# Taking turns between two output tiles in the matmuls of two ConvFFNs (one Trainium2 core, float32 trunk)

## The chip, the core and the metric

The kernel runs on one core of one Trainium2 chip. The metric is device time in microseconds (us), the median of several executions; lower is better. TensorE (PE) multiplies, VectorE (DVE) and ScalarE (ACT) do the elementwise work, GpSimd (POOL) a little of it, and SyncE (SP) issues the weight transfers. TensorE adds into PSUM, a memory of eight banks; one bank holds 512 float32 columns for each of the 128 partitions.

## The reference, cut to what matters

The program is a two-layer decoder trunk on 256 tokens with 2048 features. Each layer has a token mixer (an RG-LRU and RWKV-7 layer first, then an mLSTM layer) and after it a gated ConvFFN; a final RMSNorm closes it. The change is in the ConvFFN, which runs twice:

```python
def conv_ffn(x, norm, w_gate, w_up, conv_w, conv_b, w_down):
    h = rms_norm(x, norm)                                # 2048 features
    u = silu(causal_dwconv(h @ w_gate, conv_w, conv_b)) * (h @ w_up)   # 5632 features, 3 taps
    return x + u @ w_down
```

All of it is float32. The mixers and norms around it are unchanged.

## The kernel before

Activations lie feature-major: 128 features on the partitions, the 256 tokens along the free axis. So a product is a sum over k-tiles of 128 input features, and an output tile is 128 features by 256 tokens. A ConvFFN has 44 gate tiles and 44 up tiles over 16 k-tiles each (2048 = 16 x 128), and then 16 down tiles over 44 k-tiles each (5632 = 44 x 128): 88 x 16 + 16 x 44 = 2112 pairs of an output tile and a k-tile, 4224 in the two ConvFFNs.

Weights come in chunks of 1 MB, sixteen 128 x 128 weight tiles each. `chunk` (L192) has one transfer on the SP queue into a `raw` buffer, and splits it in four pieces of 512 columns into an exact high part `wh` (ACT, L201) and a low part `wl` (DVE, L202). There are two buffers of each, so a chunk is converted while the one before it is multiplied. The moving operand of a k-tile is stored in the same way, as [low | high], 2 x 256 columns. `mm3` (L205) makes the product of three float32r passes with two matmuls:

- a wide one (L214, for the first k-tile L211): `wh` against both halves, 512 columns into the whole bank of the output tile;
- a narrow one (L212): `wl` against the high half, 256 columns, into the second half of that bank.

For the first k-tile of an output tile the wide one comes first, since it opens the sum; for all others the narrow one comes first. Both add into the same bank, the tile `mm` of a pool of three banks (`psum_mm`, L220). So an output tile is one bank, filled by 32 matmuls (gate and up) or 88 (down) without another bank between, apart from a few side matmuls. In the even layer the products are made with `EWIDE` false: three narrow matmuls of 256 columns for a k-tile (L216 to L218).

`project` (L223) does one gate or up tile, one chunk each, and `projections` (L234) yields gate and up tiles in turn, the first two made ahead because the norm's factor `rstd` comes late. `ffn` (L363) takes them: `scaled` (L339) copies one half from PSUM by ACT (L350), adds the other by DVE (L351) and multiplies by `rstd` (L353); `conv` is one ACT and two DVE instructions (L332, L335); then come Silu (L375), the product (L377) and the split of the result into `ux` (L174, L175). `flat` (L241) does the down tiles; `add_residual` (L356) adds both halves of a finished tile onto the residual (L358, two DVE instructions) and, by `norm_tile`, prepares the next layer's operand (L269, L270) and sum of squares (L283, L285). `tick` lets side work emit a step; in a ConvFFN that is the norm's end (`np` tiles, L296 and L323) and, in the first, the folding of small weights on DVE.

A scheduler of the language sets the order on each engine when the program is built, and each engine runs its own list in that order, waiting on semaphores where a buffer or an operand is not there yet.

Of the kernel before, what the change touches and what calls it, by code (L numbers as in the profile page):

```python
"""Hybrid trunk: (RG-LRU | RWKV-7) layer, mLSTM layer, a gated ConvFFN after each, final RMSNorm.

Activations lie feature-major on the chip (128 features on the partitions, the 256 tokens along the
free axis), weights stream through in 1 MB chunks of sixteen 128x128 tiles.  The large products run
as three float32r passes over exact high/low parts of both operands; the small ones as plain float32.
"""
# [11 lines left out]
F32 = mybir.dt.float32  # L18
# [4 lines left out]
PSUM = bass.MemoryType.PSUM  # L23

P = 128
T = 256
D = 2048
# [35 lines left out]
NV = 0  # L63
# [43 lines left out]
class Builder:  # L107
# [20 lines left out]
    def load_x(self, gain, low, outs):  # L128
        """x, and the products with the low-rank inputs' weights as both come in; the first gain leads the queues"""
# [19 lines left out]
    def load_vec(self, gain):  # L149
        """the other vectors"""  # L150
        g = VOFF[gain]
        for lo, hi in ((0, g), (g + KD, NV)):
            if hi > lo:
                self.nc.sync.dma_start(out=self.vec_sb[:, lo:hi], in_=self.io["vec"][:, lo:hi])

# [16 lines left out]
    def split(self, src, x):  # L172
        """exact float32r parts of a float32 tile: x[:, 0] the low one, x[:, 1] the high one"""
# [31 lines left out]
    def mm3(self, ps, w, c, x, start, stop):  # L205
        """w x but for the product of the low parts; two halves [w_hi x_lo, w_hi x_hi + w_lo x_hi] where ps has them"""
# [16 lines left out]
    def project(self, src, wide=True):  # L223
        """one output tile of a product with the normalised residual, before the factor rstd"""
# [9 lines left out]
    def projections(self, src, n, wide=True):  # L234
        """the first two at once: the factor rstd comes late"""
# [5 lines left out]
    def flat(self, src, nk, nm, x, done):  # L241
        """products whose (m, k) tiles lie in one flat stream; done(m, psum) takes each result"""
# [30 lines left out]
    def square(self, k, engine=None):  # L273
        """onto the sum of squares: by the engine given, or by ScalarE and VectorE"""
# [41 lines left out]
    def row_bcast(self, psum, pool, cols, tag):  # L316
        """[128 tokens, 2] -> [128, 256]: the token's value on every partition"""
# [21 lines left out]
    def scaled(self, pool, ps, pad, tag, bufs=None):  # L339
        """psum * rstd behind pad zero columns"""  # L340
# [22 lines left out]
    def ffn(self, l, gain):  # L363
        nc, tc = self.nc, self.tc
        with ExitStack() as es:
            big = es.enter_context(self.tile_pool(name=f"ffn{l}", bufs=1))
            tmp = es.enter_context(self.tile_pool(name=f"ffnt{l}", bufs=2))
            nps = es.enter_context(self.tile_pool(name=f"ffn_ps{l}", bufs=2, space=PSUM))
            self.norm_psum = lambda: nps.tile([P, T], F32, name=self.name("np"), tag="np")
            ux = []  # L370
            ps = self.projections(self.io[f"fgu{l}"], 2 * NF)
            for f in range(NF):
                g = self.scaled(tmp, next(ps), 2, "g")
                c = self.conv(tmp, g, 3, f"f_conv_w{l}", NF, f"f_conv_b{l}", f, "cv")
                nc.scalar.activation(c, c, AF.Silu)  # L375
                u = self.scaled(tmp, next(ps), 0, "u")
# [3 lines left out]
            self.flat(self.io[f"fd{l}"], NF, KD, ux, lambda m, ps: self.add_residual(m, ps, gain))  # L380

# [1 line left out]
    def even(self, gain):  # L383
        nc, tc = self.nc, self.tc
        with ExitStack() as es:
# [8 lines left out]
            # low-rank inputs: [decay | a] and the gate  # L394
# [12 lines left out]
            # their parts [hi; lo] for decay and a; hi, lo and [hi; lo; hi] for the gate  # L407
# [9 lines left out]
            # the biases of halved arguments  # L417
# [24 lines left out]
            def parts(i):  # L442
                # the second half goes where spent tiles of y lie, to leave the next layer its operands' places
# [31 lines left out]
    def sigmoid(self, out, x, bias=0.0):  # L475
        """0.5 + 0.5 tanh(x / 2); the bias comes halved"""
# [663 lines left out]
```

## Time and profile before

| | |
|---|---|
| time, median of 3 runs | 2657.59 us (2653.79 to 2658.26) |
| span of the profiled execution | 2653.5 us, 4.1 us under the median |
| TensorE busy | 2612.7 us, 98% of the span, 16200 matmuls |
| TensorE weight loads | 2282.9 us, 86% |
| VectorE / ScalarE / GpSimd busy | 71% / 55% / 6% |
| DMA | 454.40 MB, 171 GB/s |
| mean granted TensorE clock | 0.997 of full speed |

Of the profiled execution the span is all that is shown. The page's busy time of TensorE counts from a matmul's start to its modelled end, and matmuls overlap; what a stream of matmuls really costs is read from the distance between starts, which the timeline gives to 0.01 us. PEld is the loading of the stationary operand, which overlaps the matmul before it. A wide matmul moves 512 columns and a narrow one 256.

### The profile page before, as it was taken

What the parts mean: (1) busy time and instruction counts of PE and PEld (TensorE: products, weight loads), DVE (VectorE), ACT (ScalarE), POOL (GpSimd) and SP (SyncE); (2) the same over time, 40 slices, a digit from 0 to 9 for tenths busy, and PEclk for the clock granted to TensorE, in tenths of its full rate; (3) what the DMA queues carried; (4) which work ended last, traced back from release to release, by engine and by line L of the source; (5) the groups of instructions that cost most, each with busy time, mean ns of one, the idle gap of its engine ahead of it and who ended that gap; (6) DMA issues with size and microseconds to landing.
All of it is one profiled execution on the core that took longest, in us unless ns stands there. A gap on an engine that the chain in (4) does not pass through costs nothing.

```text
span 2653.5 us, 42929 instructions
## 1 busy us (share of the span) xinstructions
PE 2612.7 (98%) x16200; PEld 2282.9 (86%) x16200; DVE 1890.9 (71%) x4251; ACT 1456.0 (55%) x3078; POOL 163.3 (6%) x442
## 2 busy tenths in 40 slices
PE   7999999999999999999999999999999999999997
PEld 7988887888888888888888888888888888888886
DVE  7988888897777776555777688865677777775554
ACT  5766674555555554444666667644455555554443
POOL 4122121000000000000000000000000000000000
PEclk9999999999999999999999999999999999999999
DMA  5433334565555555555444344455555555555553
GB/s 188 154 122 122 122 105 139 176 220 194 186 191 189 182 186 190 191 190 192 149 151 149 133 154 159 143 192 189 184 184 188 191 183 184 189 191 190 183 188 138
DMA packets 67120, 454.40 MB, mean 171 GB/s; under 512 B 9264, under 2 KB 9776, under 8 KB 13664
## 3 DMA queue, kind: packets, MB, share of 16 engines
q1 hardware_dynamic: 62352, 443.78, 47.9%
q0 software_dynamic: 4416, 7.85, 1.2%
q8 instruction: 128, 2.10, 0.3%
q14 instruction: 80, 0.66, 0.1%
q10 hardware_dynamic: 144, 0.01, 0.0%
HBM read 448.70 MB, written 2.10 MB: 170 GB/s over the span
## 4 chain that ended last, share of the span: by engine, by line
PE 81%; DVE 0%; ACT 0%; POOL 0%; issue 0%; DVEq 0%; POOLq 0%
PE mm L214 49%; PE mm L212 26%; PE mm L211 3%; PE sc L856 1%; PE pv L841 1%; PE pz L996 1%; PE pr L850 1%; PE pz L997 0%; DVE res L1041 0%; PE pz L974 0%; PE pt L323 0%; PE pt L1010 0%; PE pt L987 0%; DVE res L358 0%; PE pt L989 0%; POOL rsq L307 0%
## 5 line engine op out<-in xcount | busy, mean ns | idle before, releaser
L214 PE MATMUL mm<-x,wh 128*128 128x512 f32 x3600 | 1282.8, 397 | 0.0
L202 DVE TENSOR_TENSOR wl<-raw,wh 128x512 fp32r<-128x512 f32 (+1 forms) x1680 | 1100.6, 686 | 230.5 <-ACT wh L201 229.5
L201 ACT CAST wh<-raw 128x512 fp32r<-128x512 f32 (+1 forms) x1680 | 936.0, 616 | 406.9 <-PE mm L214 307.7
L212 PE MATMUL mm<-x,wl 128*128 128x256 f32 x3840 | 1045.8, 283 | 0.0
L214 PEld LDWEIGHTS mm<-x,wh 128*128 128x128 f32 x3600 | 676.3, 188 | 150.9
L212 PEld LDWEIGHTS mm<-x,wl 128*128 128x128 f32 x3840 | 725.2, 189 | 22.7 <-DVE yx L175 2.3
L214 PE MATMUL mm<-ux,wh 128*128 128x512 f32 x1376 | 484.4, 394 | 0.0
L212 PE MATMUL mm<-ux,wl 128*128 128x256 f32 x1408 | 390.4, 281 | 0.0
L214 PEld LDWEIGHTS mm<-ux,wh 128*128 128x128 f32 x1376 | 258.7, 188 | 59.6
L212 PEld LDWEIGHTS mm<-ux,wl 128*128 128x128 f32 x1408 | 264.0, 188 | 2.8
L214 PE MATMUL mm<-yx,wh 128*128 128x512 f32 x720 | 256.2, 395 | 0.0
L212 PE MATMUL mm<-yx,wl 128*128 128x256 f32 x768 | 210.3, 285 | 1.9 <-DVE wl L202 1.0
L216 PE MATMUL mm<-x,wh 128*128 128x256 f32 x640 | 194.5, 304 | 0.0
L218 PE MATMUL mm<-x,wl 128*128 128x256 f32 x640 | 182.9, 286 | 2.5 <-DVE wl L202 2.5
L217 PE MATMUL mm<-x,wh 128*128 128x256 f32 x640 | 181.5, 284 | 0.0
L350 ACT COPY g<-mm 128x256 f32<-128x256 f32 x88 | 32.9, 374 | 241.7 <-PE mm L214 241.7
L214 PEld LDWEIGHTS mm<-yx,wh 128*128 128x128 f32 x720 | 135.2, 188 | 28.8
L212 PEld LDWEIGHTS mm<-yx,wl 128*128 128x128 f32 x768 | 143.7, 188 | 7.8 <-DVE wl L202 1.4
L351 DVE TENSOR_TENSOR g<-mm,g 128x256 f32<-128x256 f32 x88 | 37.4, 425 | 138.5 <-ACT g L350 138.4
L216 PEld LDWEIGHTS mm<-x,wh 128*128 128x128 f32 x640 | 122.3, 191 | 6.9
L218 PEld LDWEIGHTS mm<-x,wl 128*128 128x128 f32 x640 | 122.5, 191 | 3.5 <-DVE wl L202 2.8
L217 PEld LDWEIGHTS mm<-x,wh 128*128 128x128 f32 x640 | 123.0, 192 | 0.4
(349 smaller groups left out, 2461.4 us busy)
## 6 DMA issues: line engine op xcount, KB each, us to landing
raw<-fgu SPq DMA_DIRECT2D x176, 1024.0 KB, 4.8
raw<-fd SPq DMA_DIRECT2D x88, 1024.0 KB, 4.8
raw<-oin SPq DMA_DIRECT2D x64, 1024.0 KB, 4.8
raw<-ein SPq DMA_DIRECT2D x40, 1024.0 KB, 4.9
raw<-oout SPq DMA_DIRECT2D x32, 1024.0 KB, 4.8
raw<-eoa SPq DMA_DIRECT2D x8, 1024.0 KB, 5.0
raw<-eob SPq DMA_DIRECT2D x8, 1024.0 KB, 4.9
wif<-wif POOLq DMA_DIRECT2D x12, 256.0 KB, 3.3
```

What stands on the lines that cost most here:

```text
L201: nc.scalar.copy(hi[:, s], raw[:, s])
L202: nc.vector.tensor_tensor(out=lo[:, s], in0=raw[:, s], in1=hi[:, s].bitcast(F32), op=ALU.subtract)
L211: TE.matmul(ps, hi, x, start=True, stop=False)
L212: TE.matmul(ps[:, 1], lo, x[:, 1], start=False, stop=False)
L214: TE.matmul(ps, hi, x, start=False, stop=stop)
L216: TE.matmul(ps, hi, x[:, 0], start=start, stop=False)
L217: TE.matmul(ps, hi, x[:, 1], start=False, stop=False)
L218: TE.matmul(ps, lo, x[:, 1], start=False, stop=stop)
L350: nc.scalar.copy(r, ps[:, 0])
L351: nc.vector.tensor_tensor(out=r, in0=ps[:, 1], in1=r, op=ALU.add)
L841: TE.matmul(ps[:, s], xm[:, 3 + s * P:3 + s * P + P], bv, start=True, stop=True)
L850: TE.matmul(ps, bl, xc, start=True, stop=True)
```

## The change

The two ConvFFNs no longer use `projections` and `flat`. A new `flat_pairs` makes two output tiles at a time: the gate and the up tile of the same 128 features, or two neighbouring down tiles. Their PSUM tile is two banks (`[P, 2, 2, T]`, 512 float32 columns for each output tile), from a pool of two such tiles, four banks; the pool of the norm's `np` tiles shrinks from two banks to one. A chunk now holds 8 k-tiles of both output tiles, so the layout of the weights in memory is changed to match on the host; its size and its number are the same. For a k-tile `mm3_pair` issues the two wide matmuls, one into each bank, and then the two narrow ones, one into each bank. The results of a pair are taken out together when the pair is done.

```diff
+    def mm3_pair(self, ps, w, c, x, start, stop):
+        TE = self.nc.tensor
+        hi = [w[0][:, i:i + P] for i in c]
+        lo = [w[1][:, i:i + P] for i in c]
+        for i in range(2):
+            TE.matmul(ps[:, i], hi[i], x, start=start, stop=False)
+        for i in range(2):
+            TE.matmul(ps[:, i, 1], lo[i], x[:, 1], start=False, stop=stop)
+
+    def flat_pairs(self, src, nk, npair, x, pool):
+        w, ps = None, None
+        for i in range(npair * nk):
+            k = i % nk
+            if i % 8 == 0:
+                w = self.chunk(src[i // 8])
+            if k == 0:
+                ps = pool.tile([P, 2, 2, T], F32, name=self.name("mp"), tag="mp")
+            c = i % 8 * 2 * P
+            self.mm3_pair(ps, w, (c, c + P), x[k], k == 0, k == nk - 1)
+            if i % 2 == 1:
+                self.tick()
+            if k == nk - 1:
+                yield ps
...
     def ffn(self, l, gain):
...
-            nps = es.enter_context(self.tile_pool(name=f"ffn_ps{l}", bufs=2, space=PSUM))
+            nps = es.enter_context(self.tile_pool(name=f"ffn_ps{l}", bufs=1, space=PSUM))
+            pps = es.enter_context(self.tile_pool(name=f"ffn_pp{l}", bufs=2, space=PSUM))
...
-            ps = self.projections(self.io[f"fgu{l}"], 2 * NF)
-            for f in range(NF):
-                g = self.scaled(tmp, next(ps), 2, "g")
+            pairs = self.flat_pairs(self.io[f"fgu{l}"], KD, NF, self.x, pps)
+
+            ahead = [next(pairs) for _ in range(2)]
+            for f, ps in enumerate(chain(ahead, pairs)):
+                g = self.scaled(tmp, ps[:, 0], 2, "g")
                 c = self.conv(tmp, g, 3, f"f_conv_w{l}", NF, f"f_conv_b{l}", f, "cv")
                 nc.scalar.activation(c, c, AF.Silu)
-                u = self.scaled(tmp, next(ps), 0, "u")
+                u = self.scaled(tmp, ps[:, 1], 0, "u")
...
-            self.flat(self.io[f"fd{l}"], NF, KD, ux, lambda m, ps: self.add_residual(m, ps, gain))
+            for m, ps in enumerate(self.flat_pairs(self.io[f"fd{l}"], NF, KD // 2, ux, pps)):
+                for i in range(2):
+                    self.add_residual(2 * m + i, ps[:, i], gain)
```

What the built programs have in a row shows the change at three places. First TensorE in the gate-and-up part of the first ConvFFN, where one output tile ends and the next begins, as it was (`mm` is an output tile's bank, `x` the operand of a k-tile, `wh` and `wl` the parts of the weights):

```order
L214 MATMUL mm_1505_9998<-x_1136_6750,wh_1503_9988 128x512
L212 MATMUL mm_1505_9998<-x_1139_6775,wl_1504_9989 128x256
L214 MATMUL mm_1505_9998<-x_1139_6775,wh_1503_9988 128x512
L211 MATMUL mm_1511_10051<-x_1073_6317,wh_1509_10041 128x512
L212 MATMUL mm_1511_10051<-x_1073_6317,wl_1510_10042 128x256
L212 MATMUL mm_1511_10051<-x_1076_6341,wl_1510_10042 128x256
L214 MATMUL mm_1511_10051<-x_1076_6341,wh_1509_10041 128x512
L212 MATMUL mm_1511_10051<-x_1082_6378,wl_1510_10042 128x256
```

and as it is now (`mp` is the tile of two banks; x2 is one matmul into each of them):

```order
L263 MATMUL mp_1493_10132<-x_1139_6775,wh_1495_10167 128x512 x2
L265 MATMUL mp_1493_10132<-x_1139_6775,wl_1496_10168 128x256 x2
L263 MATMUL mp_1504_10239<-x_1073_6317,wh_1502_10229 128x512 x2
L265 MATMUL mp_1504_10239<-x_1073_6317,wl_1503_10230 128x256 x2
L263 MATMUL mp_1504_10239<-x_1076_6341,wh_1502_10229 128x512 x2
L265 MATMUL mp_1504_10239<-x_1076_6341,wl_1503_10230 128x256 x2
```

Narrow and wide ones alternated; now two wide ones and two narrow ones follow each other. The number of matmuls and of weight loads is the same.

Second, VectorE in the same part, as it was: one gate tile's results and one up tile's, with the conversion of a chunk (`wl`) after each:

```order
L351 TENSOR_TENSOR g_1512_10084<-mm_1511_10051,g_1512_10084 128x256
L353 TENSOR_TENSOR g_1512_10084<-g_1512_10084,bc_1155_6897 128x256
L202 TENSOR_TENSOR wl_1522_10150<-raw_1520_10147,wh_1521_10149 128x512 x2
L335 SCALAR_TENSOR_TENSOR cv_1513_10089<-g_1512_10084,vec_sb_70,cv_1513_10089 128x256
L202 TENSOR_TENSOR wl_1522_10150<-raw_1520_10147,wh_1521_10149 128x512
L335 SCALAR_TENSOR_TENSOR cv_1513_10089<-g_1512_10084,vec_sb_70,cv_1513_10089 128x256
L202 TENSOR_TENSOR wl_1522_10150<-raw_1520_10147,wh_1521_10149 128x512
L351 TENSOR_TENSOR u_1518_10139<-mm_1517_10106,u_1518_10139 128x256
L353 TENSOR_TENSOR u_1518_10139<-u_1518_10139,bc_1155_6897 128x256
L202 TENSOR_TENSOR wl_1528_10205<-raw_1526_10202,wh_1527_10204 128x512
L377 TENSOR_TENSOR u_1518_10139<-u_1518_10139,cv_1513_10089 128x256
```

and as it is now:

```order
L202 TENSOR_TENSOR wl_1496_10168<-raw_1494_10165,wh_1495_10167 128x512
L377 TENSOR_TENSOR g_1486_10102<-mp_1482_10025,g_1486_10102 128x256
L202 TENSOR_TENSOR wl_1496_10168<-raw_1494_10165,wh_1495_10167 128x512
L379 TENSOR_TENSOR g_1486_10102<-g_1486_10102,bc_1154_6899 128x256
L377 TENSOR_TENSOR u_1488_10112<-mp_1482_10025,u_1488_10112 128x256
L202 TENSOR_TENSOR wl_1496_10168<-raw_1494_10165,wh_1495_10167 128x512
L361 SCALAR_TENSOR_TENSOR cv_1487_10107<-g_1486_10102,vec_sb_70,cv_1487_10107 128x256
L379 TENSOR_TENSOR u_1488_10112<-u_1488_10112,bc_1154_6899 128x256
L361 SCALAR_TENSOR_TENSOR cv_1487_10107<-g_1486_10102,vec_sb_70,cv_1487_10107 128x256
L202 TENSOR_TENSOR wl_1496_10168<-raw_1494_10165,wh_1495_10167 128x512
L406 TENSOR_TENSOR u_1488_10112<-u_1488_10112,cv_1487_10107 128x256
L202 TENSOR_TENSOR wl_1503_10230<-raw_1501_10227,wh_1502_10229 128x512
```

The work on both output tiles now lies between the pieces of one chunk, the second chunk of the next pair, where it was spread over the conversions of two chunks.

Third, VectorE at the very end of the second ConvFFN, as it was:

```order
L202 TENSOR_TENSOR wl_3475_26946<-raw_3473_26943,wh_3474_26945 128x512 x4
L358 TENSOR_TENSOR res_97<-mm_3469_26874,res_97 128x256 x2
L285 TENSOR_TENSOR ssq_3323_25073<-ssq_3323_25073,sq_3476_26989 128x256
L299 TENSOR_SCALAR ms_3478_26999<-mm_3477_26996 128x2
L322 TENSOR_SCALAR dg_3481_27004<-con_sb_71,rsq_3479_27001 128x128
```

and as it is now:

```order
L202 TENSOR_TENSOR wl_3370_26843<-raw_3368_26840,wh_3369_26842 128x512 x4
L384 TENSOR_TENSOR res_97<-mp_3355_26647,res_97 128x256 x4
L311 TENSOR_TENSOR ssq_3236_25108<-ssq_3236_25108,sq_3371_26886 128x256
L311 TENSOR_TENSOR ssq_3236_25108<-ssq_3236_25108,sq_3372_26892 128x256
L325 TENSOR_SCALAR ms_3374_26903<-mm_3373_26900 128x2
```

Two output tiles end together, so four additions and two sums of squares stand there in place of two and one.

## Rows read from the trace of the kernel before

**Rows 1.** The page: busy time of each engine with its share of the span, and the chain that ended last, by engine and by line.

```profile
PE 2612.7 (98%) x16200; PEld 2282.9 (86%) x16200; DVE 1890.9 (71%) x4251; ACT 1456.0 (55%) x3078; POOL 163.3 (6%) x442
...
PE mm L214 49%; PE mm L212 26%; PE mm L211 3%; PE sc L856 1%; PE pv L841 1%; PE pz L996 1%; PE pr L850 1%; PE pz L997 0%; DVE res L1041 0%; PE pz L974 0%; PE pt L323 0%; PE pt L1010 0%; PE pt L987 0%; DVE res L358 0%; PE pt L989 0%; POOL rsq L307 0%
```

**Rows 2.** Busy time in four stretches (us from the span's start, first the stretch and its length): gate and up of the first ConvFFN, its down product, and the same two of the second. Columns: PE, PEld, DVE, ACT, POOL with instructions in brackets, granted clock, DMA share, GB/s.

```profile
514.29:1011.97 497.68, 497.68 (x2825) 432.44 (x2824) 372.89 (x773) 273.50 (x576) 11.45 (x55) 1.00 0.56 194
1011.97:1258.98 247.01, 247.01 (x1410) 215.81 (x1409) 134.26 (x239) 108.16 (x208) 0.90 (x5) 1.00 0.55 190
1892.85:2390.44 497.59, 497.59 (x2826) 432.41 (x2824) 352.16 (x707) 270.61 (x573) 5.29 (x43) 1.00 0.53 186
2390.44:2637.44 247.00, 247.00 (x1409) 215.67 (x1407) 126.11 (x220) 107.30 (x204) 0.00 (x0) 1.00 0.51 179
```

**Rows 3.** The chain that ended last, in order of time (start, length): the norm's own matmuls at the start of the first ConvFFN.

```profile
521.51 0.34 PE np L296 x4
524.77 0.44 PE np L323 x4
```

**Rows 4.** Timeline of TensorE in the gate and up part (start us, length us to the modelled end), over nine k-tiles and into the next output tile.

```profile
703.64 0.40 PE L214 MATMUL mm<-x,wh 128*128 128x512 f32 x1
...
706.34 0.28 PE L212 MATMUL mm<-x,wl 128*128 128x256 f32 x1
706.46 0.40 PE L214 MATMUL mm<-x,wh 128*128 128x512 f32 x1
706.70 0.28 PE L212 MATMUL mm<-x,wl 128*128 128x256 f32 x1
706.82 0.40 PE L214 MATMUL mm<-x,wh 128*128 128x512 f32 x1
707.05 0.39 PE L211 MATMUL mm<-x,wh 128*128 128x512 f32 x1
707.28 0.40 PE L212 MATMUL mm<-x,wl 128*128 128x256 f32 x2
707.51 0.40 PE L214 MATMUL mm<-x,wh 128*128 128x512 f32 x1
```

**Rows 5.** Timeline of TensorE: the first two output tiles of the mLSTM layer's projection begin (16 k-tiles, nothing else between).

```profile
1258.98 0.40 PE L211 MATMUL mm<-x,wh 128*128 128x512 f32 x1
...
1264.53 0.39 PE L211 MATMUL mm<-x,wh 128*128 128x512 f32 x1
```

**Rows 6.** Timeline of TensorE in the even layer, narrow matmuls alone: the first and the last of 37 that follow each other.

```profile
50.44 0.28 PE L216 MATMUL mm<-x,wh 128*128 128x256 f32 x1
...
54.75 0.28 PE L216 MATMUL mm<-x,wh 128*128 128x256 f32 x1
```

**Rows 7.** Timeline of TensorE at three more beginnings of an output tile (gate and up; down of the first ConvFFN; down of the second): the last wide matmul of the tile before, and the first L214 of the new tile, four matmuls later.

```profile
599.53 0.40 PE L214 MATMUL mm<-x,wh 128*128 128x512 f32 x1
...
600.23 0.40 PE L214 MATMUL mm<-x,wh 128*128 128x512 f32 x1
...
1042.63 0.39 PE L214 MATMUL mm<-ux,wh 128*128 128x512 f32 x1
...
1043.32 0.39 PE L214 MATMUL mm<-ux,wh 128*128 128x512 f32 x1
...
2405.74 0.40 PE L214 MATMUL mm<-ux,wh 128*128 128x512 f32 x1
...
2406.45 0.39 PE L214 MATMUL mm<-ux,wh 128*128 128x512 f32 x1
```

**Rows 8.** Timeline of TensorE in the mLSTM layer: a wide matmul, then side matmuls into another bank (`pv`).

```profile
1279.18 0.40 PE L214 MATMUL mm<-x,wh 128*128 128x512 f32 x1
1279.41 0.66 PE L841 MATMUL pv<-bv,xm 128*128 128x145 f32 x4
```

**Rows 9.** Timeline of the weight loads (PEld) in the gate and up part: the load for a wide matmul and the one for the narrow matmul after it.

```profile
706.34 0.19 PEld L214 LDWEIGHTS mm<-x,wh 128*128 128x128 f32 x1
...
706.46 0.19 PEld L212 LDWEIGHTS mm<-x,wl 128*128 128x128 f32 x1
```

**Rows 10.** Timeline of ScalarE and of VectorE after a gate tile's end at 712.70.

```profile
712.95 0.37 ACT L350 COPY g<-mm 128x256 f32<-128x256 f32 x1 [2.94 <-PE mm L214]
713.22 1.14 ACT L201 CAST wh<-raw 128x512 fp32r<-128x512 f32 x2
...
713.36 0.42 DVE L351 TENSOR_TENSOR g<-mm,g 128x256 f32<-128x256 f32 x1 [1.74 <-ACT g L350]
714.16 1.29 DVE L202 TENSOR_TENSOR wl<-raw,wh 128x512 fp32r<-128x512 f32 x2
```

**Rows 11.** Timeline of VectorE where the first ConvFFN ends and the mLSTM layer begins.

```profile
1259.17 0.88 DVE L358 TENSOR_TENSOR res<-mm,res 128x256 f32<-128x256 f32 x2 [2.43 <-PE mm L214]
1259.97 1.28 DVE L202 TENSOR_TENSOR wl<-raw,wh 128x512 fp32r<-128x512 f32 x2
1261.18 0.48 DVE L270 SCALAR_TENSOR_TENSOR x<-res,vec_sb,x 128x256 fp32r<-128x256 f32 x1
```

**Rows 12.** Timeline after the last wide matmul of the second ConvFFN.

```profile
2637.64 0.88 DVE L358 TENSOR_TENSOR res<-mm,res 128x256 f32<-128x256 f32 x2 [8.01 <-PE mm L214]
2638.55 0.42 ACT L283 ACTIVATE sq<-res 128x256 f32<-128x256 f32 x1 [9.89 <-DVE res L358]
2639.00 0.43 DVE L285 TENSOR_TENSOR ssq<-ssq,sq 128x256 f32<-128x256 f32 x1 [0.48 <-ACT sq L283]
...
2639.57 0.58 PE L296 MATMUL mm<-con_sb,ssq 128*128 128x1 f32 x4 [1.98 <-DVE ssq L285]
```

More of the change, by code (lines that the diff above doesn't have):

```diff
@@ L1063, in _flat, with _pairs @@
     return np.ascontiguousarray(t.transpose(0, 2, 1, 3)).reshape(-1, P, 2048)
+def _pairs(ws):
+    n, k, _, _ = ws.shape
+    t = ws.reshape(n, k // P, P, 2, P).transpose(0, 1, 3, 2, 4).reshape(-1, 16, P, P)
+    return np.ascontiguousarray(t.transpose(0, 2, 1, 3)).reshape(-1, P, 2048)
 def _feat(v):
@@ L1092, in _arrange @@
     for l in range(2):
-        gu = np.empty((NF, 2, P, D), np.float32)
-        gu[:, 0], gu[:, 1] = _by_cols(I["ffn_w_gate"][l]), _by_cols(I["ffn_w_up"][l])
-        o[f"fgu{l}"] = gu.reshape(2 * NF, P, D)
-        o[f"fd{l}"] = _flat(I["ffn_w_down"][l])
+        by = lambda n: I[n][l].reshape(D, NF, P).transpose(1, 0, 2)
+        o[f"fgu{l}"] = _pairs(np.stack([by("ffn_w_gate"), by("ffn_w_up")], 2))
+        o[f"fd{l}"] = _pairs(I["ffn_w_down"][l].reshape(DFF, KD // 2, 2, P).transpose(1, 0, 2, 3))
     lora = z(8, P, 4, P)
```

## The prediction

> **What bounds the kernel now.** I read the page first. TensorE is busy 98% of the span, and the chain that ended last runs almost wholly through the wide (L214) and narrow (L212) matmuls [rows 1]. Then I cut the span where the ConvFFNs begin and end. Their four stretches hold 497.68, 247.01, 497.59 and 247.00 us, 1489.3 us or 56% of the span. In each of them TensorE is busy for the whole stretch and the granted clock is 1.00, the 2.4 GHz level, while VectorE and ScalarE are busy for 51 to 75% and 43 to 55% [rows 2]. So nothing is waited for there: the stage costs as many matmuls as it has, times the distance between their starts. About 0.8 us of a gate-and-up stretch are the norm's own matmuls [rows 3]. Without them, a pair of output tiles costs for one k-tile, four matmuls, (497.64 - 0.78) / 704 = 0.7058 us in gate and up, and 247.0 / 352 = 0.7017 us in down.
>
> Is there anything to gain in these 0.70 us? Three states of the same kind of stream stand in the trace.
> - Gate and up: nine k-tiles take 706.82 - 703.64 = 3.18 us, 0.3533 us for a wide and a narrow one [rows 4].
> - The first tile of the mLSTM layer: sixteen k-tiles of the same alternation take 5.55 us, 0.347 us each [rows 5]. The stream can run faster with nothing changed in it.
> - The even layer: 36 steps of narrow matmuls take 4.31 us, 0.1197 us each [rows 6].
>
> A wide one in the short state then costs 0.347 - 0.120 = 0.227 us, and 256 columns more cost 0.108 us. That is 2.4 columns a ns, and leaves 0.012 us with each matmul that no column accounts for. In gate and up it is more: 6 x 0.1067 us = 0.640 us for the 1536 columns of four matmuls at that rate, so 0.066 us over four matmuls, 0.016 us each. The change can earn only what is in these 0.016 us, at most 0.066 x 1408 + 0.062 x 704 = 136 us.
>
> **The change part by part.**
>
> *Another bank for each matmul.* The trace already has such steps. When an output tile ends, its last wide matmul is followed by a wide one into a new bank: 706.82 to 707.05, 0.23 us. Inside the tile the step from a wide one to a narrow one into the same bank is 0.24 us (706.46 to 706.70) [rows 4]. From a wide one to `pv`, another bank again, it is 0.23 us [rows 8]. If matmuls waited for their own bank, these steps would have lost some 0.02 us; they lose at most what the last digit hides. I take 0 for the change of bank alone; the other end, all of the 0.016 us, is a rival below.
>
> *Wide, wide, narrow, narrow.* This is the part that I expect to matter. The beginning of every output tile has exactly the new sequence once: the last wide of the old tile, the first wide of the new, two narrow ones, then the next wide. It takes 707.51 - 706.82 = 0.69 us [rows 4], and at three more places 0.70, 0.69 and 0.71 us [rows 7]; the mean is 0.6975 us, each read to some 0.01 us. At the short state's price, two wides and two narrows cost 2 x 0.347 = 0.694 us [rows 5]. Both are under 0.7058 and 0.7017. I take 0.694, since it is the price of a stream that goes on, where a beginning is one step among others, and the mean of the beginnings is near it. The ends are 0.680 (the shortest beginning less the reading error) and 0.7058 (the alternation's long state stays).
> Gate and up: 704 x (0.7058 - 0.694) = 8.3 us; down: 352 x (0.7017 - 0.694) = 2.7 us. For two ConvFFNs that is 22.0 us.
>
> *Weight loads.* There are as many as before. Each begins with the matmul ahead of it and lasts 0.19 us [rows 9], yet narrow matmuls follow each other in 0.12 us [rows 6], so two narrow ones in a row are no new demand. I take 0; what it costs if that fails is the slower rival.
> The Trainium skill ("TensorE: Matmul & The Clock Gate", LDWEIGHTS) gives a load's time as its columns over 1.2 GHz, 107 ns for 128 columns, which just fits under a narrow matmul. No run here shows that figure by itself, and it would leave this term at 0 too.
>
> *Results taken out in pairs.* After a pair, VectorE has the results of both tiles between the four pieces of one chunk. Before, the two came 5.65 us apart. That work's cover: the chunk being converted is the second of the next pair, and TensorE first works through the pair's first chunk, 8 x 0.694 = 5.55 us. A piece's cast takes 0.6 us and its subtraction 0.65 us [rows 10]. So the first piece is ready some 1.3 us after the pair's end, and the fourth about 4 x 0.65 us plus the six other instructions at 0.42 us plus that first cast, 5.7 us. They are wanted at 5.55 and, a quarter of a chunk (1.39 us) apart, at 9.7 us. VectorE's whole load is 352 / 44 = 8.0 us for a pair that lasts 11.1 us [rows 2], and 8.5 us with the folding of the first ConvFFN. I cost it at 0. Without that cover each of the 88 pairs could lose up to 1 us. The two-bank tiles are just as roomy as the three banks: a bank must be empty one pair, 11.1 us, after its end, and two tiles, 11.3 us, before.
>
> *The end of the first ConvFFN.* Two tiles end together, and the mLSTM layer's second chunk is converted between them. Until the operand of k-tile 15 is ready VectorE has four additions at 0.40, four pieces at 0.60, two operands at 0.4 to 0.5 and one sum of squares at 0.34 us: about 5.3 us, from 0.2 us after the tile's start [rows 11]. TensorE wants it after 15 x 0.347 + 0.12 = 5.3 us. I take 0.2 us, between 0 and 1.
>
> *The end of the second ConvFFN.* The chain there is two additions (0.88), a square (0.42), a sum (0.43), then the norm's matmul [rows 12]. Two more additions stand ahead of it: 0.9 us more, nothing hides them.
>
> **Sum.** -22.0 + 0.2 + 0.9 = -20.9 us. The span of 2653.5 us becomes 2632.6 us. It lies 4.1 us under the median of the runs, so I put the difference on the median: 2657.6 - 20.9 = 2636.7 us.
>
> **The rivals.**
>
> *The long state stays.* The alternation costs 0.3533 us in one stretch and 0.347 us in another without a difference in the code, so the price depends on how a stream settles, and the new one may settle in its own long state at 0.700 to 0.708 us. A beginning with 0.71 us [rows 7] speaks for it; three others of 0.69 to 0.70 us speak against. With 0.7058 and 0.7017 kept, only 1.1 us come on top: 2659 us.
>
> *Two narrow ones in a row are held by the weight loads; slower.* The narrow ones would cost 0.1197 us [rows 6], where loads follow each other most closely, and the wide ones keep the long state's 0.3533 - 0.118 = 0.2353 us. Together 0.710 us: +4.2 ns x 1408 and +8.3 ns x 704 are 11.8 us, with 1.1 us 2670 us. It decides from a pair of (1487.6 - 1.1) / 2112 = 0.7038 us upwards. Against it: at all beginnings but one the sum was under that.
>
> *The bank is the reason after all.* The 0.016 us go, four matmuls cost 0.640 us, and 136 - 1 us are saved: 2523 us. Partial gains between that and my low end belong here. For it there is only that the long state is unexplained; against it, the steps into another bank.
> The Trainium skill (the same page, Back-to-back issue gap) has isolated matmuls follow each other after their columns at 2.4 GHz plus 2.5 ns, which makes 0.650 us for the four and 2544 us. The trace differs by far: 0.69 us at the least, also where the bank changes.
>
> *The results in pairs stall TensorE.* A late piece of `wl` would show as waits of TensorE on VectorE, up to some tens of us in 88 pairs. The slack of 4 us speaks against.
>
> **How the numbers follow.** A measurement of this kernel can tell about 0.2%, 5.3 us, from no change. Forecast 0.60; long state 0.19, nearly all of it within 0.2%; narrow ones held 0.12; bank 0.05; stalls 0.04. A pair must come under 0.7013 us to be faster by 5.3 us. The forecast's and the bank's chances and a little of the long state's make faster 0.67; same 0.16; slower 0.17. The range begins at 0.680 us a pair, 2112 x 0.680 = 1436.2 in place of 1487.6 us, so 2657.6 - 51.4 + 1.1 = 2607 us, which leaves out the bank's 0.05. It ends at 2667 us, past the long state, and leaves out most of the two slower cases.
>
> **What would show it.** In the profile after: the four stretches at about 489.4, 244.3, 489.4 and 244.3 us, with TensorE busy throughout at clock 1.00; starts of four matmuls 0.694 us apart; a wide-to-wide step of 0.23 us, not 0.215 us. If the bank matters, both steps shrink at once. If the results in pairs hurt, TensorE's idle time names VectorE or ScalarE. If the narrow ones are held, their steps are 0.12 us while the wide ones stay at 0.235 us. The weak point is the sustained price of a sequence which the trace shows only once per output tile.

## The result and the profile after

The changed kernel takes 2637.14 us, the median of 4 runs (2636.45 to 2638.66); the kernel before takes 2657.56 us (4 runs, 2653.79 to 2658.26). The ratio is 0.9928, 95% interval 0.9916 to 0.994: 20.4 us less, outside the 0.2% that a measurement of this kernel can tell. The prediction was 2636.7 us.

The page of the changed kernel, the lines that answer to [rows 1]:

```profile
PE 2595.7 (98%) x16200; PEld 2274.7 (86%) x16200; DVE 1872.8 (71%) x4251; ACT 1457.9 (55%) x3078; POOL 163.7 (6%) x442
...
PE mp L263 37%; PE mp L265 19%; PE mm L214 14%; PE mm L212 7%; PE sc L887 1%; PE mm L211 1%; PE pv L872 1%; PE pz L1027 1%; PE pr L881 1%; PE pz L1028 0%; DVE res L1072 0%; PE pz L1005 0%; PE pt L349 0%; PE pt L1041 0%; PE pt L1018 0%; DVE res L384 0%
```

The chain still runs through TensorE alone. In the ConvFFNs it now passes the wide ones of line 263 and the narrow ones of line 265; what is left of lines 211, 212 and 214 is the mixers. No other engine took a share.

Busy time in the same four stretches as [rows 2], with the same columns:

```profile
516.75:1008.09 491.34, 491.34 (x2825) 428.82 (x2824) 364.15 (x769) 272.44 (x572) 11.40 (x55) 1.00 0.55 197
1008.09:1251.01 242.92, 242.92 (x1410) 213.86 (x1409) 133.21 (x239) 108.89 (x210) 1.23 (x8) 1.00 0.54 192
1885.19:2376.52 491.33, 491.33 (x2825) 428.83 (x2824) 342.46 (x703) 270.60 (x570) 5.24 (x43) 1.00 0.53 189
2376.52:2619.44 242.92, 242.92 (x1410) 213.84 (x1408) 125.24 (x221) 107.53 (x205) 0.00 (x0) 1.00 0.50 181
```

Read length and PE first: they are equal in every row, as before, at a granted clock of 1.00, the 2.4 GHz level. So nothing is waited for and only the distance between matmuls changed. Against [rows 2] the stretches lost 6.34, 4.09, 6.26 and 4.08 us, together 20.8 us. Four matmuls cost (491.34 - 0.78) / 704 = 0.6968 us in gate and up (before 0.7058) and 242.92 / 352 = 0.6901 us in down (before 0.7017).

The timeline of TensorE in gate and up (start, length to the modelled end; x2 is two matmuls in a row, one into each bank):

```profile
703.65 0.63 PE L263 MATMUL mp<-x,wh 128*128 128x512 f32 x2
704.12 0.39 PE L265 MATMUL mp<-x,wl 128*128 128x256 f32 x2
704.35 0.63 PE L263 MATMUL mp<-x,wh 128*128 128x512 f32 x2
...
706.43 0.40 PE L263 MATMUL mp<-x,wh 128*128 128x512 f32 x1
```

Two wide ones take 704.12 - 703.65 = 0.47 us and two narrow ones 0.23 us; four k-tiles take 706.43 - 703.65 = 2.78 us. In these rows, read to 0.01 us, a wide step is about 0.235 us and a narrow one about 0.115 us.

The two small terms of the prediction can be read too. First the waits where the first ConvFFN ends (engine, what it waited for, us in total, times, longest), then the timeline of the end of the second ConvFFN, as in [rows 12]:

```profile
PEld mm L214 <- DVE x L296: 0.2, 1, 0.2
```

```profile
2619.64 1.67 DVE L384 TENSOR_TENSOR res<-mp,res 128x256 f32<-128x256 f32 x4 [8.12 <-PE mp L265]
...
2622.33 0.75 PE L322 MATMUL mm<-con_sb,ssq 128*128 128x1 f32 x4 [2.73 <-DVE ssq L311]
```

Four additions take 1.67 us where two took 0.88, and TensorE waits 2.73 us for the last sum of squares where it waited 1.98.

The spans differ by 2653.5 - 2636.9 = 16.6 us, less than the medians. Ahead of the first ConvFFN 2.46 us were lost, where no code changed; 0.31 us between the two ConvFFNs and 1.4 us behind the second make up the rest. Of the 1.4 us, 0.75 us are the wait just shown. Most of the remainder lies in the final norm's last matmuls: the windows show a granted clock of 0.58 for the changed kernel (2622.0 to 2626.0) and 0.91 for the kernel before at the same place (2639.4 to 2643.0). Whether the longer wait brought that on was not tested; the kernel with the order alone, which has no pairs, shows 0.74 there (2619.0 to 2624.0).

In the even layer's output product TensorE ran for some microseconds at the 1.2 GHz level. Here are the windows of this stretch (the columns as above), first of the changed kernel, then of the kernel before:

```profile
475.00:480.00 5.00, 3.86 (x11) 2.88 (x12) 3.38 (x9) 2.89 (x7) 0.81 (x2) 0.57 0.29 93
480.00:485.00 5.00, 5.00 (x24) 4.31 (x23) 4.16 (x11) 3.48 (x9) 0.00 (x0) 0.75 0.00 0
```

```profile
475.00:480.00 5.00, 3.62 (x18) 2.86 (x19) 3.94 (x11) 3.60 (x9) 0.75 (x2) 1.00 0.31 93
480.00:485.00 5.00, 5.00 (x30) 4.39 (x29) 4.97 (x13) 3.91 (x9) 0.00 (x0) 1.00 0.12 20
```

TensorE idles for more than a microsecond there in both; in one execution the granted clock fell behind it, in the other not. Among the profiles below such a stretch is missing in the kernel with the banks alone, which has the pairs, and stands in the one with the wide matmul first everywhere, which has none; so I do not count it as a part of the change.

### The profile page after: what moved, and what is told of

It reads as the page before. It is cut to its first block, busy times and chain, and to the rows that moved or that the text cites. A ratio compares the mean times of both kernels' runs of the same rounds, so it can differ in the third digit from the quotient of the medians.

```text
span 2636.9 us, 42747 instructions
## 1 busy us (share of the span) xinstructions
PE 2595.7 (98%) x16200; PEld 2274.7 (86%) x16200; DVE 1872.8 (71%) x4251; ACT 1457.9 (55%) x3078; POOL 163.7 (6%) x442
## 4 chain that ended last, share of the span: by engine, by line
PE 81%; DVE 0%; ACT 0%; POOL 0%; issue 0%; DVEq 0%; POOLq 0%
PE mp L263 37%; PE mp L265 19%; PE mm L214 14%; PE mm L212 7%; PE sc L887 1%; PE mm L211 1%; PE pv L872 1%; PE pz L1027 1%; PE pr L881 1%; PE pz L1028 0%; DVE res L1072 0%; PE pz L1005 0%; PE pt L349 0%; PE pt L1041 0%; PE pt L1018 0%; DVE res L384 0%
## 5 line engine op out<-in xcount | busy, mean ns | idle before, releaser
L263 PE MATMUL mp<-x,wh 128*128 128x512 f32 x2816 | 884.7, 395 | 0.0
L265 PEld LDWEIGHTS mp<-x,wl 128*128 128x128 f32 x2816 | 529.0, 188 | 125.0
L265 PE MATMUL mp<-x,wl 128*128 128x256 f32 x2816 | 553.2, 278 | 0.0
L263 PE MATMUL mp<-ux,wh 128*128 128x512 f32 x1408 | 436.8, 392 | 0.0
L263 PEld LDWEIGHTS mp<-x,wh 128*128 128x128 f32 x2816 | 428.8, 189 | 0.1
L214 PE MATMUL mm<-x,wh 128*128 128x512 f32 x960 | 341.7, 394 | 0.0
L212 PE MATMUL mm<-x,wl 128*128 128x256 f32 x1024 | 283.4, 287 | 0.0
L265 PE MATMUL mp<-ux,wl 128*128 128x256 f32 x1408 | 277.8, 279 | 0.0
L214 PE MATMUL mm<-yx,wh 128*128 128x512 f32 x720 | 258.2, 398 | 0.0
L214 PEld LDWEIGHTS mm<-x,wh 128*128 128x128 f32 x960 | 180.2, 188 | 35.9 <-DVE x L296 0.2
L212 PEld LDWEIGHTS mm<-x,wl 128*128 128x128 f32 x1024 | 193.2, 189 | 7.5 <-DVE yx L175 2.3
L218 PE MATMUL mm<-x,wl 128*128 128x256 f32 x640 | 182.9, 286 | 2.3 <-DVE wl L202 2.3
L214 PEld LDWEIGHTS mm<-yx,wh 128*128 128x128 f32 x720 | 136.4, 190 | 29.2 <-DVE yx L175 0.2
L216 PEld LDWEIGHTS mm<-x,wh 128*128 128x128 f32 x640 | 122.4, 191 | 6.9
```

The source lines that it names most:

```text
L212: TE.matmul(ps[:, 1], lo, x[:, 1], start=False, stop=False)
L214: TE.matmul(ps, hi, x, start=False, stop=stop)
L216: TE.matmul(ps, hi, x[:, 0], start=start, stop=False)
L218: TE.matmul(ps, lo, x[:, 1], start=False, stop=stop)
L263: TE.matmul(ps[:, i], hi[i], x, start=start, stop=False)
L265: TE.matmul(ps[:, i, 1], lo[i], x[:, 1], start=False, stop=stop)
```

## The experiments

What is to be told apart: does the gain come from the **order** (wide, wide, narrow, narrow), from the **banks**, or from neither, since alternation itself has a short and a long state? The times stand beside runs of the kernel before on the same chip.

**The order alone.** The kernel before, one output tile and one bank at a time; two k-tiles are grouped.

```diff
+    def mm3_two(self, ps, w, c, xs, start, stop):
+        TE = self.nc.tensor
+        for i in range(2):
+            TE.matmul(ps, w[0][:, c + i * P:c + i * P + P], xs[i], start=start and i == 0, stop=False)
+        for i in range(2):
+            TE.matmul(ps[:, 1], w[1][:, c + i * P:c + i * P + P], xs[i][:, 1], start=False, stop=stop and i == 1)
...
```

> The kernel before, but in both ConvFFNs the matmuls of two neighbouring k-tiles of one output tile are grouped: two wide, then two narrow, all into the same bank. No matmul changes its bank inside an output tile, and nothing is paired. Order theory: the four stretches shrink as in the changed kernel, gate and up from 497.6 to about 491 us, down from 247.0 to about 243 us; without the work in pairs at the end about 1 us less than the changed kernel, 2636 us. Bank theory: every matmul still adds into the bank of the one before it, so the stretches stay at 497.6 and 247.0 us and the time at 2657.6 us.

It took 2635.29 us (5 runs, 2633.65 to 2636.93), ratio 0.9923 (0.9911 to 0.9936). Its windows, first ConvFFN and gate and up of the second:

```profile
515.73:1007.08 491.35, 491.35 (x2826) 428.82 (x2825) 369.34 (x773) 279.49 (x575) 11.43 (x55) 1.00 0.57 197
1007.08:1249.99 242.91, 242.91 (x1410) 213.74 (x1409) 134.16 (x239) 108.33 (x209) 0.77 (x3) 1.00 0.55 193
1883.99:2375.35 491.36, 491.36 (x2826) 428.82 (x2825) 347.62 (x707) 278.73 (x573) 5.28 (x43) 1.00 0.54 189
```

These are the changed kernel's stretches to within 0.03 us, without a second bank, without pairs of output tiles and with the old layout of the weights. The order is enough for the whole gain. It does away with two things at once, though: the alternation of the widths, and the break wide, narrow, narrow, wide at the beginning of each output tile. The run under "Alternation without the break" below takes away the break and keeps the alternation.

**The banks alone.** The changed kernel; each k-tile goes wide a, narrow a, wide b, narrow b (a and b are the two banks), which is alternation again.

```diff
         for i in range(2):
             TE.matmul(ps[:, i], hi[i], x, start=start, stop=False)
-        for i in range(2):
             TE.matmul(ps[:, i, 1], lo[i], x[:, 1], start=False, stop=stop)
```

> The changed kernel with its pairs, its two-bank tiles and its layout, but for each k-tile wide and narrow of the first output tile, then wide and narrow of the second, so the widths alternate as in the kernel before while every second matmul changes the bank. Order theory: the price of the alternation, 0.70 to 0.706 us for four matmuls, stretches of 494 to 498 and 244 to 247 us, time 2646 to 2659 us with about 1 us for the ends of the pairs. Bank theory: half of the steps change the bank, so at least half of the 20.4 us of the changed kernel, 2647 us, with the gain all in those steps: narrow to wide 0.110 us or less, wide to narrow unchanged.

It took 2647.63 us (5 runs: 2640.21, 2648.4, 2647.63, 2639.9, 2649.45), ratio 0.9964 (0.9951 to 0.9978), 8.3 us under the kernel before beside it (2655.96 us), two fifths of the gain and the time that the bank theory had named. Its windows:

```profile
514.40:1003.58 489.18, 489.18 (x2825) 427.83 (x2824) 364.19 (x769) 272.29 (x572) 11.41 (x55) 1.00 0.57 198
1003.58:1249.21 245.63, 245.63 (x1411) 215.13 (x1409) 132.97 (x239) 108.59 (x209) 1.25 (x8) 1.00 0.55 190
1883.38:2372.51 489.13, 489.13 (x2825) 431.26 (x2824) 342.44 (x703) 270.44 (x570) 5.30 (x43) 1.00 0.54 189
2372.51:2621.15 248.64, 248.64 (x1410) 216.69 (x1408) 125.48 (x221) 106.90 (x205) 0.00 (x0) 1.00 0.51 178
```

That alternation is always slow falls with this: here it takes 489.2 us in gate and up, 2.2 us less than the changed kernel, and in one of the two down stretches 248.64 us, more than before. But this kernel differs from before in three things: banks, pairs, and that each output tile no longer begins with the break wide, narrow, narrow, wide. The next runs separate them.

**The bank by itself, in a stream of one width.** The narrow matmul is made wide, so that the low part of the weights is multiplied by both halves of the operand; the products of two low parts are added, which the computation has nowhere else. All matmuls in the ConvFFNs then have 512 columns. Once in the kernel before (one bank for all matmuls of an output tile):

```diff
-            TE.matmul(ps[:, 1], lo, x[:, 1], start=False, stop=False)
+            if self.all_wide:
+                TE.matmul(ps, lo, x, start=False, stop=False)
+            else:
+                TE.matmul(ps[:, 1], lo, x[:, 1], start=False, stop=False)
...
```

and once in the changed kernel (another bank for each matmul):

```diff
-            TE.matmul(ps[:, i, 1], lo[i], x[:, 1], start=False, stop=stop)
+            TE.matmul(ps[:, i], lo[i], x, start=False, stop=stop)
```

> The kernel before with the narrow matmul of the ConvFFNs made wide (the low weights times both halves, which adds the product of the two low parts that the kernel leaves out). All matmuls of an output tile are equal and add into one bank. Order theory: 0.227 to 0.236 us a step, so 640 to 665 us for the 88 output tiles of gate and up, and the same to within 1% as with changing banks. Bank theory: 0.235 us a step, and clearly more than with changing banks.

> The changed kernel with the narrow matmuls made wide in the same way: all matmuls equal, each into the other bank than the one before it. Order theory: the same step as with one bank, 0.227 to 0.236 us, the whole time within 1% of that kernel. Bank theory: 0.216 us a step, 8% or some 130 us less over the two ConvFFNs.

One run each: 3087.99 us with one bank, 3097.29 us with two. The windows, first with one bank, then with two:

```profile
512.95:1152.24 639.29, 639.29 (x2825) 529.42 (x2824) 374.99 (x773) 272.46 (x575) 11.78 (x55) 1.00 0.44 151
1152.24:1474.54 322.30, 322.30 (x1410) 264.44 (x1409) 134.65 (x239) 108.63 (x208) 1.01 (x6) 1.00 0.42 147
2108.53:2747.85 639.32, 639.32 (x2825) 529.42 (x2824) 351.71 (x707) 270.72 (x573) 5.28 (x43) 1.00 0.42 145
2747.85:3069.91 322.06, 322.06 (x1408) 264.25 (x1407) 126.18 (x220) 107.59 (x204) 0.00 (x0) 1.00 0.39 136
```

```profile
516.87:1159.77 642.90, 639.92 (x2826) 529.43 (x2824) 369.39 (x772) 278.28 (x577) 11.75 (x55) 1.00 0.44 152
1159.77:1482.06 322.29, 322.29 (x1409) 264.43 (x1408) 133.14 (x239) 109.08 (x210) 1.45 (x9) 1.00 0.42 145
2116.20:2755.51 639.31, 639.31 (x2825) 529.60 (x2824) 346.44 (x703) 275.24 (x571) 5.23 (x43) 1.00 0.42 146
2755.51:3077.58 322.07, 322.07 (x1409) 264.24 (x1407) 125.42 (x221) 107.87 (x205) 0.00 (x0) 1.00 0.38 134
```

Three stretches agree within 0.01 us over 1408 to 2816 matmuls: in a stream of one width the bank costs and saves nothing that shows. In the first stretch PE's busy time is 3.0 us under the length, and the waits of that stretch name why; the timeline of VectorE shows what stood ahead of the late piece:

```profile
PE mp L265 <- DVE wl L202: 3.0, 2, 2.0
```

```profile
597.93 0.69 DVE L948 TENSOR_TENSOR wif<-wif,wqkv 128x512 f32<-128x512 f32 x1 [4.01 <-DMA wif<-wif]
598.53 0.69 DVE L202 TENSOR_TENSOR wl<-raw,wh 128x512 fp32r<-128x512 f32 x1
```

VectorE stood 4.01 us at a folding step that waited for a small transfer, and the weight piece queued behind it came late. This happened twice in one execution, and not in the profile of the changed kernel. The rest of the 9.3 us between the two lies outside these four stretches and is not followed up.

**Alternation without the break.** The kernel before with one edit in `mm3`: in the ConvFFNs the wide matmul comes first for every k-tile. One bank, no pairs.

```diff
-            if start:
-                TE.matmul(ps, hi, x, start=True, stop=False)
-            TE.matmul(ps[:, 1], lo, x[:, 1], start=False, stop=False)
-            if not start:
+            first = start or self.wide_first
+            if first:
+                TE.matmul(ps, hi, x, start=start, stop=False)
+            TE.matmul(ps[:, 1], lo, x[:, 1], start=False, stop=first and stop)
+            if not first:
...
```

> The kernel before, with one edit: in the two ConvFFNs the wide matmul comes first for every k-tile of an output tile, not for the first alone. One output tile at a time, one bank, the same chunks; the stream is then wide, narrow, wide, narrow without the break wide, narrow, narrow, wide that each output tile began with. Theory A (a strictly alternating stream settles by itself in a short or a long state, and the break at each tile's start drove the stream of before into the long one): stretches of 488 to 492 us (gate and up) and 243 to 249 us (down) in place of 497.6 and 247.0, the time 2638 to 2650 us, with a spread over its runs as wide as that of the alternating kernel with two banks (2639.9 to 2649.45). Theory B (that kernel was faster than before by its two banks or by its pairs): 497.6 and 247.0 us, 2656 us. Theory C (alternation is long wherever it stands): 2656 us or more.

It took 2648.14 us (7 runs, 2639.36 to 2652.48), ratio 0.9968 (0.9956 to 0.9979). The windows of the profiled execution:

```profile
514.32:1003.51 489.19, 489.19 (x2826) 427.86 (x2824) 369.44 (x773) 279.47 (x575) 11.39 (x55) 1.00 0.57 198
1003.51:1249.13 245.62, 245.62 (x1411) 215.13 (x1409) 134.25 (x239) 108.25 (x208) 0.90 (x5) 1.00 0.55 191
1883.27:2381.59 498.32, 498.32 (x2825) 432.21 (x2824) 347.80 (x707) 278.84 (x573) 5.24 (x43) 1.00 0.53 186
2381.59:2630.22 248.63, 248.63 (x1410) 216.50 (x1408) 125.83 (x220) 107.43 (x204) 0.00 (x0) 1.00 0.50 178
```

The first and the third row are the same code in the same execution, with TensorE busy throughout at the same clock, and 9.1 us apart. Seven wide and narrow ones of the one and of the other, in the timeline of TensorE:

```profile
799.67 0.39 PE L213 MATMUL mm<-x,wh 128*128 128x512 f32 x1
...
802.09 0.40 PE L213 MATMUL mm<-x,wh 128*128 128x512 f32 x1
```

```profile
2199.62 0.40 PE L213 MATMUL mm<-x,wh 128*128 128x512 f32 x1
...
2202.09 0.40 PE L213 MATMUL mm<-x,wh 128*128 128x512 f32 x1
```

2.42 us and 2.47 us: 0.346 us for a wide and a narrow one in the first, 0.353 us in the second. So alternation settles at one of several prices. Banks and pairs were not what made the kernel with the banks alone faster: with neither, the first two stretches are the same 489.19 and 245.62 us, and the time is the same.

**Where the price changes.** The traces of the kernel before and of the last one show it. First the kernel before, at the first wide matmul of three neighbouring down tiles of the first ConvFFN:

```profile
1011.97 0.39 PE L211 MATMUL mm<-ux,wh 128*128 128x512 f32 x1
...
1027.51 0.39 PE L211 MATMUL mm<-ux,wh 128*128 128x512 f32 x1
...
1042.86 0.39 PE L211 MATMUL mm<-ux,wh 128*128 128x512 f32 x1
```

The first tile takes 15.54 us and the second 15.35 us for the same 88 matmuls, 0.706 and 0.698 us for four. It goes on like that, 15.53 and 15.35 us in turn, through all sixteen down tiles of both ConvFFNs. Inside a tile the price stays; it changes with the break at the next tile's beginning. So the 0.7017 us of the down stretches is the mean of two prices. In gate and up the break does not go both ways; here are three neighbouring tiles near the beginning of the first ConvFFN:

```profile
526.44 0.40 PE L211 MATMUL mm<-x,wh 128*128 128x512 f32 x1
...
532.00 0.39 PE L211 MATMUL mm<-x,wh 128*128 128x512 f32 x1
...
537.65 0.39 PE L211 MATMUL mm<-x,wh 128*128 128x512 f32 x1
```

One tile takes 5.56 us, the next 5.65 us, and all that follow in the stretch keep 5.65 us. Second, the kernel with the wide matmul first, whose tiles begin without a break, in gate and up of its first ConvFFN:

```profile
514.67 0.40 PE L213 MATMUL mm<-x,wh 128*128 128x512 f32 x1
...
521.03 0.40 PE L213 MATMUL mm<-x,wh 128*128 128x512 f32 x1
...
521.39 0.50 PE L298 MATMUL np<-con_sb,ssq 128*128 128x1 f32 x4
```

Eighteen k-tiles take 6.36 us, 0.353 us each: this stretch began at the long price too. Then come the norm's own matmuls (`np`) between two k-tiles, four at 521.39 and four more at 524.66, and behind them a k-tile takes 0.347 us to the end of the stretch. In the second ConvFFN the stream is long ahead of them and long again behind them. So inside a stretch a price lasts until something interrupts the sequence, and each interruption can pick another. From gate and up to down it also changes where the sequence goes on and only the operand's tiles are others (`ux` for `x`): 489.19 us are 0.694 us for four matmuls and 245.62 us are 0.698 us. The traces show where a price changes, and not why.

**The same in every product.** As the last one, with `wide_first` set in the mixers' wide products as well.

> As the kernel with the wide matmul first for every k-tile of the ConvFFNs, but in every product with wide matmuls (the mLSTM layer's two projections and the output product of the even layer too). Theory A: the same gain in the ConvFFNs and up to 1.7% of the wide time elsewhere, 2630 to 2650 us. Theories B and C: 2656 us or more.

2644.44 us (4 runs, 2644.12 to 2651.91), ratio 0.9963 (0.995 to 0.9976). Its windows: gate and up and down of the first ConvFFN, then gate and up of the second.

```profile
515.76:1004.77 489.01, 489.01 (x2827) 431.21 (x2826) 369.34 (x773) 279.41 (x575) 11.38 (x55) 1.00 0.57 198
1004.77:1253.52 248.75, 248.75 (x1411) 216.84 (x1409) 134.25 (x239) 108.25 (x208) 0.91 (x5) 1.00 0.54 188
1887.97:2376.98 489.01, 489.01 (x2827) 431.21 (x2826) 347.73 (x707) 278.78 (x573) 5.23 (x43) 1.00 0.54 189
```

Both gate and up stretches are in the short state this time, and the down stretch is long, 3.1 us more than the same code took in the run above. So the order within the stretch does not decide which one is met.

**Wide, wide, narrow, narrow in every product.** The kernel with the order alone, with `mm3_two` in the mLSTM layer's two projections and the even layer's output product too.

> The kernel before with the order wide, wide, narrow, narrow over two k-tiles of one output tile, one bank, in every product with wide matmuls: the ConvFFNs (as in the kernel with the order alone, 2635.29 us), the two projections of the mLSTM layer and the even layer's output product. If order is all there is, each wide and narrow pair outside the ConvFFNs gets the same 0.0044 to 0.0021 us that the gate and up and the down part got; there are 34 output tiles of 16 k-tiles in the mLSTM input part counted at least and 16 of 32 in its output part, 16 of 16 in the even layer's: some 1300 pairs, 3 to 6 us less, 2629 to 2633 us. Rival: the other products have side matmuls between them that break the stream up already, and nothing is gained: 2635 us.

2635.84 us (4 runs, 2633.8 to 2637.34), ratio 0.9923 (0.9911 to 0.9936): no more than in the ConvFFNs alone (2635.29 us). The windows: the mLSTM layer's input part, its output part, and the even layer's output product.

```profile
1252.29:1704.62 452.33, 452.20 (x2642) 395.80 (x2641) 343.05 (x869) 299.88 (x676) 30.06 (x104) 1.00 0.43 150
1704.62:1883.11 178.49, 178.27 (x1035) 156.42 (x1034) 109.13 (x213) 82.96 (x167) 0.84 (x3) 1.00 0.53 187
389.06:518.01 128.95, 122.15 (x825) 97.15 (x823) 107.48 (x282) 63.50 (x140) 13.42 (x22) 0.99 0.39 132
```

In the kernel before the same three took 452.36, 181.51 and 125.17 us. The output part, a plain stream, gained 3.0 us on its 512 pairs, 0.0059 us each; that is what the down parts gained, 4.1 / 704 = 0.0058 us, and not the 0.0021 us that the expectation had put for them; the input part, with side matmuls between, gained nothing; the even layer's product lost 3.8 us in this execution, which has a stretch at a lower granted clock there. Whether that loss belongs to the order was not separated.

**Four and four.** The changed kernel with four wide and then four narrow matmuls, over two k-tiles of the two output tiles.

```diff
+        at = lambda j, i: slice(c + (2 * j + i) * P, c + (2 * j + i + 1) * P)
+        for j in range(2):
+            for i in range(2):
+                TE.matmul(ps[:, i], w[0][:, at(j, i)], xs[j], start=start and j == 0, stop=False)
+        for j in range(2):
+            for i in range(2):
+                TE.matmul(ps[:, i, 1], w[1][:, at(j, i)], xs[j][:, 1], start=False, stop=stop and j == 1)
...
```

> The changed kernel with four wide matmuls in a row and then four narrow ones (two k-tiles of the same two output tiles). If each change between the widths costs something, half as many changes give a part of it back: the four matmuls of a k-tile took 0.6968 us (gate and up) and 0.690 us (down); a pure wide stream has 0.2264 us a matmul and a pure narrow one 0.120, which makes 0.6928. So gate and up may gain 4 us each and down lose 1: 2630 to 2636 us. Rival: the order of two and two is as good as any: 2637 us. [...]

2644.86 us (4 runs, 2643.88 to 2646.29), ratio 0.9958 (0.9945 to 0.9971): 7.7 us over the changed kernel. The windows of the first ConvFFN:

```profile
515.93:1010.76 494.83, 494.83 (x2825) 432.54 (x2824) 364.35 (x769) 272.92 (x573) 11.41 (x55) 1.00 0.56 196
1010.76:1254.27 243.51, 243.51 (x1411) 213.57 (x1409) 132.90 (x239) 108.54 (x210) 0.78 (x4) 1.00 0.56 192
```

Neither the expectation nor its rival came true: gate and up lost 3.5 us and down 0.6 us, so fewer changes of width are not cheaper, and two and two is not as good as any. TensorE was never idle in these stretches, so four narrow ones in a row did not make it wait. It is one more order with a price of its own, 0.7018 us for two wide and two narrow ones in gate and up and 0.6918 us in down.

## Why the prediction was right

- **What bounds the kernel** was read rightly: TensorE's stream, by the distance between matmuls. Four stretches lost 20.8 us of a predicted 22.0.
- **The bank at nothing** is shown: the order alone reaches the whole gain with one bank, and with wide matmuls alone three stretches agree within 0.01 us. The rival with 2523 us is out. The Trainium skill ("TensorE: Matmul & The Clock Gate", Back-to-back issue gap), whose isolated gap of 512/2.4 + 2.5 = 216 ns stood beside that rival, is not met in this float32r stream even with wide ones alone: (639.29 - 0.78) / 2816 = 0.2267 us in gate and up, 322.30 / 1408 = 0.2289 us in down.
- **Wide, wide, narrow, narrow at 0.694 us** named the right cause, the order, and mis-sized two terms. Gate and up came at 0.6968 us, saving 6.3 us a ConvFFN and not 8.3; down at 0.6901 us, saving 4.1 us and not 2.7. I had chosen the sum of the short state's prices over what the beginnings of the tiles showed. The beginnings' mean, 0.6975 us, would have done better in gate and up and worse in down. Neither is the price of the new order, which has its own in gate and up and another in down; 0.694 us was taken over from a different sequence. The two errors have opposite signs and left 1.2 us. So it is in part luck that the forecast came within 0.5 us of the measured median.
- **The long state** was a rival at 2659 us. It is out as a result, but its premise was right: the same alternation cost 489.19 and 498.32 us in one execution. What the prediction took as one price in down, 0.7017 us, was the long and the short one in turn from tile to tile; the rows it read did not show that, though the trace held it. With the break at each tile's start gone, alternation costs 2639.36 to 2652.48 us. With the break, the kernel before stayed between 2653.94 and 2657.95 us in 12 runs beside these. Its trace agrees: the break re-picks the price at every tile, in gate and up the long one each time after the third tile, in down the long and the short one in turn. Without the break, alternation came to 2648.14 us in the median, 8 us under the kernel before beside it, but not steadily. The new order, which has no such break either, showed the same prices in every profile.
- **What no column accounts for** was put at 0.012 us a matmul in the short state and 0.016 us in the long one, at two slightly different rates. At the rate of the second, 0.1067 us for 256 columns, the first is (0.694 - 0.640) / 4 = 0.0135 us. The forecast does not rest on it.
- **Two narrow ones in a row** are not held: 0.23 us for two, and four in a row do not make TensorE idle. The slower rival is out.
- **The results in pairs** cost nothing: TensorE is busy for the whole length of all four stretches. The two-bank tiles held too.
- **The ends** came at 0.2 us (predicted 0.2) and 2.73 - 1.98 = 0.75 us (predicted 0.9). Some 0.6 us more behind the second ConvFFN, with the lower clock there, were not in the sum.

What stays open is why one order has several prices, and why an interruption picks the one or the other. Left alone, a price holds for hundreds of microseconds, over many chunks, with the clock at the same level. The load of VectorE and ScalarE does not pick it: gate and up of the second ConvFFN took 498.32 us in one run and 489.01 us in another, with VectorE busy for 347.80 and 347.73 us and ScalarE for 278.84 and 278.78 us. None of the runs shows the cause. Nor was it separated how much of the gain of wide, wide, narrow, narrow belongs to the sequence itself and how much to the break that it lacks.

## What to carry to other kernels

When TensorE is busy throughout and the clock is at its upper level, compare the distance between matmuls in all stretches of the same shape before planning anything, and tile by tile inside them: two prices for the same sequence say that a gain of about that size may lie in the order alone. Look at what interrupts the sequence where the price changes. Before restructuring tiles and layouts for a suspected cause, try the cheapest kernel that has the cause alone; here a few lines that group two k-tiles gave the whole gain of a change to pools, weights and epilogues. The order that kept its prices here gave runs within 3.6 us of each other, alternation without the break runs up to 13 us apart, so judge an order of matmuls by several runs and by each stretch, never by one profile.

## What was not expected of the hardware

- One sequence of matmuls, in one execution, at one clock, has prices that differ by 1.9% (489.19 and 498.32 us for 2816 matmuls), each kept from the norm's own matmuls to the stretch's end.
- In the kernel before, the same 88 matmuls take 15.53 and 15.35 us in turn from one down tile to the next.
- Matmuls of one width are not free of it: 512 columns cost 0.2267 us each in gate and up and 0.2289 us in down, with one bank or with two.
- Longer runs of one width are not better: two and two took 491.34 us in gate and up, four and four 494.83 us, and strict alternation 489.01 to 498.32 us.
